# A decoder block whose FFN is multiplied by Strassen's seven products: other signs, sums of h made one stage earlier, operands of f made between products

## The chip, the cores and the metric

One core of one Trainium2 chip runs the whole program. The metric is the device time of one execution in microseconds (us). The names of the engines in the rows are PE (TensorE, matrix products), PEld (its weight loads), DVE (VectorE), ACT (ScalarE), POOL (GpSimd) and SP (SyncE, whose queue issues the DMAs here). PSUM is the memory into which PE writes its sums, SBUF the one in which everything else lies.

## What is computed

One decoder layer on a sequence of 1024 tokens with 1024 channels, in float32. An attention branch and an mLSTM branch run on the same normalised input, are gated, added and multiplied with w_out. Then comes the part that the change is about, a dense FFN with 2816 inner channels, and a last norm:

```python
x = x + (jax.nn.sigmoid(ga) * ya + jax.nn.sigmoid(gm) * ym) @ w_out
f = rmsnorm(x, norm2_g)
h = jax.nn.silu(f @ w_ffn_gate) * (f @ w_ffn_up)
x = x + h @ w_ffn_down
out = rmsnorm(x, final_norm_g)
```

## The kernel before

Every product is made exact enough by splitting both operands into a high and a low half (`split`, L71 to L73): ACT rounds the source into the high tile, DVE subtracts it from the source to give the low tile, and PE does three matmuls, high by high, high by low and low by high (`three`, L828 to L831). One matmul is 128x128 by 128x512.

The program goes through stages. Up to about 657 us it does the projections, the two branches and the product with w_out (loop at L762, eight channel blocks j, each in two token halves). Each half is added to x (L772), scaled into a tile of F_ (L773, f without the row factor) and transposed to tokens (`to_tokens`, L713), where the squares for the norm are summed (ACT L732, DVE L734) and x is written to a DRAM tile x2d.

The FFN uses the Winograd form of Strassen's scheme: a product of two matrices cut into 2x2 quarters is done with seven products in place of eight, at the price of sums and differences of quarters beforehand and of results afterwards.

**Gate and up.** There are 22 pairs n (two channel blocks each; even n are gate, odd n are up). For each pair the seven products run in the order 1, 6, 5, 7, 2, 3, 4 (ORDER, L794). Each is 4 blocks of K by three matmuls, so 12 matmuls, and 84 for a pair. The operands of f for the seven products are 28 tiles z (`f_split` L750, `f_raw` L755, `f_t` L895). They are the same for all pairs and stay resident. Products 1, 2 and 3 take quarters of f as they are; 4, 5, 6 and 7 take differences. Before the first product two of the four K blocks of 1, 2, 3 have been made; everything else, and two passes over differences, stands in the program between the last product with w_out and the first of gate (L915 to L928). The operands of the weights are made 4 products ahead (LA, `prep`, L806): POOL forms four sums per pair (L814), then a split. Weight pairs are loaded by `load_pair` (L800), one pair ahead. Results go out of PSUM by ACT (L867, L875) and DVE (L871, L879, L890); `done` (L842) multiplies by the row factor Rt and applies Silu for gate, multiplies gate by up for up, and stores the quarter of h in the DRAM tile hd_ (L850). The row factor needs rstd2, which comes from the sums of squares (L929 and a power on POOL, L141) and is spread over partitions by PE (`rows_of`, L143).

**Down.** Seven passes over the 11 blocks p, in the order 1, 5, 2, 3, 6, 7, 4 (DORD, L935), 77 steps c of 12 matmuls (4 token blocks t by three). `dload` (L954, 5 steps ahead) fetches quarters of h and of w_dn, `dprep` (L978, 3 steps ahead) forms the sums on POOL (`op`, L984: none in passes 1 and 2, two per step in 5, 3 and 7, one in 6 and 4) and splits the two operands, 512 wide each. Passes 2 and 3 add into the PSUM banks of passes 1 and 5. After each pass the four banks are taken out: ACT copies after 1, 5 and 3; after 2 DVE adds into the rows of x (`add_r`, L1030); after 6 and 7 DVE adds bank and earlier result, POOL adds the next (L1110, L1117). `square` (L1039, ACT) sums squares, `by_g3` (L1058) multiplies by the last norm's weights, `finish` (L1042) takes the power on POOL (L1046) and scales and stores. Pass 4 begins with eight `add_r` on DVE and four `by_g3` on POOL for the second half of the tokens (L1070), and does its last four steps bank by bank.

Instructions are put in order for each engine by the tile framework: among those whose inputs it expects to be there, the one that stands first in the program goes first. On the chip each engine's queue then runs in that order. Tiles of 1024 floats come from one pool `blk` of 37 buffers, half tiles from pools named ev and ws; a tile waits until a buffer has been released.

Of the kernel before, what the change touches and what calls it, by code (L numbers as in the profile page):

```python
# [15 lines left out]
P = 128  # L16
# [16 lines left out]
def hybrid_block(ctx, tc, xT, xt, par, g3row, cst, abias, w_fm, w_mv, w_br, w_o, w_gu, w_dn, out):  # L33
# [675 lines left out]
    hd_ = dr.tile([NF, P, S], F32, name="hd_")  # L709
# [33 lines left out]

    fz = {i: [None] * 4 for i in range(1, 8)}
# [10 lines left out]
    def f_raw(kt):  # L755
        (z11, z12), (z21, z22) = halves(F_[2 * kt]), halves(F_[2 * kt + 1])
        f_split(1, kt, z11)
        f_split(2, kt, z21)
        f_split(3, kt, z22)

    later = []
    for j in range(KD):  # L762
# [6 lines left out]
        g = prm[:, C_G2 + j:C_G2 + j + 1]  # L769
        for h in range(2):  # L770
# [6 lines left out]
        if j in (3, 5):  # L777
            f_raw(j // 2 - 1)
    rstd2 = cp.tile([P, 8], F32, name="rstd2")
    ph_b.close()  # L780
    pC = ctx.enter_context(tc.tile_pool(name="pC", bufs=1))

    def half(name, tag, bufs):
        return pC.tile([P, HALF], F32, name=name, tag=tag, bufs=bufs)

    def bank(s, i):
        if i == 3:
            return st_ps()
        if s == 0:
            return pm.tile([P, HALF], F32, name="mm", tag="mm", bufs=3)  # L790
        return pb.tile([P, HALF], F32, name="mb", tag="mb", bufs=3)


    ORDER = (1, 6, 5, 7, 2, 3, 4)  # L794
    NP2 = NF // 2
    NG7 = 2 * NP2 * 7
    LA = 4
    raws, hl, sums = {}, {}, {}

    def load_pair(n):  # L800

        raws[n] = [blk("wr2") for _ in range(2)]
        for i in range(2):
            nc.sync.dma_start(out=raws[n][i], in_=w_gu[n, i])

    def prep(g):  # L806
        n, i = g // 7, ORDER[g % 7]
        if g % 7 == 0 and n + 1 < 2 * NP2:
            load_pair(n + 1)
        (x11, x12), (x21, x22) = halves(raws[n][0]), halves(raws[n][1])  # L810

        def s_(name, a, b, op):
            sums[name] = half("s_", "ws", 5)
            G.tensor_tensor(sums[name], a, b, op)  # L814
        if i == 6:
            s_(5, x21, x22, ALU.add)
            s_(6, sums[5], x11, ALU.subtract)
        elif i == 7:
            s_(7, x11, x21, ALU.subtract)
        elif i == 3:  # L820
            s_(3, x12, sums[6], ALU.subtract)
        src = {1: x11, 2: x12, 4: x22}
        hi = wp.tile([P, HALF], F32R, name="whi", tag="whi", bufs=5)
        lo = wp.tile([P, HALF], F32R, name="wlo", tag="wlo", bufs=5)
        split(hi, lo, src[i] if i in src else sums[i])
        hl[g] = (hi, lo)
# [6 lines left out]
    def seven(ps, g, more=False):  # L833
        hi, lo = hl.pop(g)
        for kt in range(4):
            c = slice(kt * P, (kt + 1) * P)
            zh, zl = halves(fz[ORDER[g % 7]][kt])
            three(ps, hi[:, c], lo[:, c], zh, zl, kt == 0 and not more, kt == 3, more)

    sg = {}  # L840

    def done(n, ij, c):  # L842
# [9 lines left out]
    def pair(n, also):  # L852
        s, b, e = n % 2, {}, {}
        if s == 0:
            sg.update(enumerate(x for _ in range(2) for x in halves(blk("sg"))))

        def ev(name):
            e[name] = half(name, "ev", 7)
            return e[name]
        for q, i in enumerate(ORDER):  # L860
            g = n * 7 + q
            if g + LA < NG7:
                prep(g + LA)
            if i == 1:
# [49 lines left out]
    for g in range(LA):  # L914
        prep(g)  # L915
# [280 lines left out]
```

## Time and profile before

| | us |
|---|---|
| median of three runs (1390.23 to 1393.22) | 1390.87 |
| the profiled execution | 1392.68 |
| its span, first to last instruction | 1390.9 |
| up to the first product of gate | 657.2 |
| gate and up | 454.6 |
| down, to the last matmul | 271.6 |
| from there to the end | 7.5 |

The page begins with the busy time of each engine and the granted clock of PE in 40 slices of the span. A busy PE is not a PE at its pace: a matmul at the lower clock counts as busy too. So the stages are best read by asking how long they would take if every matmul followed the one before at the full pace, and how much longer they took.

### The profile page before, as it was taken

To read this page: it belongs to the slowest core of one execution; us is meant where nothing else is said; L and a number is where in the kernel's file an instruction comes from. 1 tells how busy PE (TensorE), PEld (TensorE's weight loads), DVE (VectorE), ACT (ScalarE), POOL (GpSimd) and SP (SyncE) were. 2 spreads that over 40 slices of the span, in tenths; PEclk is the share of its full clock that TensorE was granted. 3 is DMA by queue.
4 is the path that set the end of the run, shared out by engine and by line. 5 is a ranking of instruction groups with operands and counts; after the bars stand their busy time and mean duration, and the time that the engine had idled before them with its cause. 6 is when DMAs were issued, how large, how long until landed. Compare 5 with 4: busy or idle time off the path is not lost.

```text
span 1390.9 us, 16876 instructions
## 1 busy us (share of the span) xinstructions
PE 1321.1 (95%) x6090; PEld 1073.8 (77%) x6090; DVE 752.7 (54%) x1290; ACT 571.5 (41%) x1134; POOL 522.0 (38%) x437
## 2 busy tenths in 40 slices
PE   9999999999999999999599999999999998998874
PEld 6888997778888888887488888888888776876653
DVE  6469663565344444334865444544455366656656
ACT  5379863565122222243533333333333243525232
POOL 0245442210000000101465444555455159275966
PEclk9999999999999999999699999999999999998986
DMA  9111011001202111143221222222220295854461
GB/s 336 48 46 32 16 31 61 31 24 33 66 25 60 46 46 54 61 151 127 98 86 61 83 76 92 91 76 91 91 76 32 83 342 173 284 169 146 144 219 61
DMA packets 56964, 134.47 MB, mean 97 GB/s; under 512 B 6449, under 2 KB 6705, under 8 KB 56881
## 3 DMA queue, kind: packets, MB, share of 16 engines
q1 hardware_dynamic: 56880, 133.39, 28.8%
q8 instruction: 48, 0.79, 0.2%
q14 instruction: 36, 0.29, 0.1%
HBM read 113.45 MB, written 19.92 MB: 96 GB/s over the span
## 4 chain that ended last, share of the span: by engine, by line
PE 77%; POOL 7%; DVE 7%; DMA 4%; issue 3%; ACT 1%; SPq 1%; POOLq 0%; ACTq 0%; DVEq 0%
PE mm L108 7%; PE mm L110 7%; PE mm L109 7%; PE mm L830 5%; PE mm L831 5%; PE mm L829 4%; PE mb L830 4%; PE mb L831 4%; PE mb L829 4%; PE mb L110 4%; PE mb L109 4%; PE mb L108 4%; PE st L829 3%; PE st L830 3%; PE st L831 3%
## 5 line engine op out<-in xcount | busy, mean ns | idle before, releaser
L108 PE MATMUL mm<-uh,whi 128*128 128x512 f32 x352 | 140.0, 400 | 0.9 <-ACT whi L72 0.9
L110 PE MATMUL mm<-uh,wlo 128*128 128x512 f32 x352 | 139.0, 395 | 0.0
L109 PE MATMUL mm<-ul,whi 128*128 128x512 f32 x352 | 138.7, 394 | 0.0
L72 ACT ACTIVATE whi<-wraw 128x512 fp32r<-128x512 f32 (+1 forms) x100 | 61.7, 628 | 159.4 <-PE mb L109 99.8
L829 PE MATMUL mm<-z,whi 128*128 128x512 f32 x220 | 88.3, 402 | 7.9 <-ACT z L72 7.9
L880 POOL TENSOR_TENSOR w<-w,d 128x512 f32<-128x512 f32 x22 | 35.3, 1605 | 153.3 <-DVE w L879 147.2
L901 POOL TENSOR_TENSOR t__5803<-f 128x512 f32<-128x512 f32 x1 | 1.3, 1304 | 242.0 <-ACT f L773 242.0
L830 PE MATMUL mm<-z,whi 128*128 128x512 f32 x220 | 88.2, 402 | 3.2 <-DVE z L73 3.2
L831 PE MATMUL mm<-z,wlo 128*128 128x512 f32 x220 | 87.6, 399 | 0.0
L831 PE MATMUL mb<-z,wlo 128*128 128x512 f32 x220 | 86.7, 394 | 0.0
L830 PE MATMUL mb<-z,whi 128*128 128x512 f32 x220 | 86.7, 394 | 0.0
L829 PE MATMUL mb<-z,whi 128*128 128x512 f32 x220 | 86.7, 394 | 0.0
L72 ACT ACTIVATE whi<-wr 128x512 fp32r<-128x512 f32 x66 | 41.5, 629 | 94.7 <-PE st L830 40.9
L108 PEld LDWEIGHTS mm<-uh,whi 128*128 128x128 f32 x352 | 66.3, 188 | 17.0 <-ACT whi L72 2.1
L110 PEld LDWEIGHTS mm<-uh,wlo 128*128 128x128 f32 x352 | 66.2, 188 | 15.5 <-DVE wlo L73 0.2
L109 PEld LDWEIGHTS mm<-ul,whi 128*128 128x128 f32 x352 | 66.3, 188 | 14.4
L73 DVE TENSOR_TENSOR wlo<-wraw,whi 128x512 fp32r<-128x512 f32 (+1 forms) x72 | 48.8, 688 | 51.7 <-ACT whi L72 51.7
L73 DVE TENSOR_TENSOR wlo<-wr,whi 128x512 fp32r<-128x512 f32 x66 | 53.0, 804 | 42.1 <-ACT whi L72 42.1
L830 PE MATMUL mm<-xz 128*128 128x512 f32 x132 | 56.3, 427 | 18.7 <-DVE xz L73 18.7
L829 PE MATMUL st<-z,whi 128*128 128x512 f32 x176 | 70.4, 400 | 0.0
L830 PE MATMUL st<-z,whi 128*128 128x512 f32 x176 | 69.9, 397 | 0.0
L831 PE MATMUL st<-z,wlo 128*128 128x512 f32 x176 | 69.7, 396 | 0.0
(653 smaller groups left out, 3644.1 us busy)
## 6 DMA issues: line engine op xcount, KB each, us to landing
wr<-in_w_gu_dram SPq DMA_DIRECT2D x44, 512.0 KB, 3.8
ld<-in_w_dn_dram SPq DMA_DIRECT2D x88, 256.0 KB, 3.6
wraw<-in_w_fm_dram SPq DMA_DIRECT2D x28, 512.0 KB, 3.6
ld<-hd__5018 SPq DMA_DIRECT2D x55, 256.0 KB, 3.9
hd__5018<-sg SPq DMA_DIRECT2D x44, 256.0 KB, 2.2
xr<-in_xT_dram SPq DMA_DIRECT2D x14, 512.0 KB, 3.7
xt<-in_xt_dram SPq DMA_DIRECT2D x8, 512.0 KB, 7.5
wraw<-in_w_br_dram SPq DMA_DIRECT2D x16, 256.0 KB, 2.7
```

What stands on the lines that cost most here:

```text
L72: A.activation(hi, src, AF.Copy)
L73: eng.tensor_tensor(lo, src, hi.bitcast(F32), ALU.subtract)
L108: T.matmul(ps, ah, bh, start=(i == 0), stop=False)
L109: T.matmul(ps, ah, bl, start=False, stop=False)
L110: T.matmul(ps, al, bh, start=False, stop=(i == n - 1))
L829: T.matmul(ps, xh, zh, start=start, stop=False, skip_group_check=more)
L830: T.matmul(ps, xh, zl, start=False, stop=False, skip_group_check=more)
L831: T.matmul(ps, xl, zh, start=False, stop=stop, skip_group_check=more)
L880: G.tensor_tensor(e["w"], e["w"], e["d5"], ALU.add)
L901: eng.tensor_tensor(ts_[k, kt], a, b, ALU.subtract)
```

## The change

Signs are turned so that other quarters become differences: products 1, 2 and 3 of gate and up still take quarters of f, 5 takes z11 - z12, 6 that plus z22, 4 takes z21 minus that, 7 takes z12 - z22, all made in place in F_. The weights' four POOL sums per pair are all additions now.

The operands of f are made in another place. Of the K blocks 0 to 2, those for products 1 and 5 are made during the product with w_out (`f_even`), the last block of 1 too. Behind it come the last block of 5 and the four of 6; those of 7, 2, 3 and 4 are made two at a time after the first eight products. The first two pairs are interleaved: their products 1 and 5, then 6 and 7, then 2, 3 and 4 follow each other pair by pair. Pair 0 is loaded during the last block of w_out. The rows of rstd2 are spread after product 7 of pair 0, in place of a spot before its `done`.

The sums of h that down needs are formed once when a quarter set is finished (`h_sums`): three on POOL, one on DVE, and all seven operands are stored, each quarter 128x512. `done` gives one more product to DVE and no longer stores the second quarter. In down each step loads one operand of h, ready made, beside one or two quarters of w_dn; POOL does one sum per step in passes 5, 6, 7 and 4, ACT one copy in 5 and 6. Both operands lie in one tile of 1024, which is split at once. Loads are 6 steps ahead and operands 4. The first four are loaded and made during the last products of up. After passes 6 and 7 all sums are on DVE; `by_g3` is gone, and `finish` does scale and weight in one DVE instruction for each half.

```diff
-    hd_ = dr.tile([NF, P, S], F32, name="hd_")
+    hd_ = dr.tile([7, NF // 2, P, HALF], F32, name="hd_")
...
+    def f_even(kt):
+        z11, z12 = halves(F_[2 * kt])
         f_split(1, kt, z11)
-        f_split(2, kt, z21)
-        f_split(3, kt, z22)
+        f_t(5, kt, z11, z11, z12, ALU.subtract)
+
+    def f_t(i, kt, dst, a, b, op):
+        (V if kt % 2 else G).tensor_tensor(dst, a, b, op)
+        f_split(i, kt, dst)
...
+    SEQ = [(n, i) for i2 in ((1, 5), (6, 7), (2, 3, 4)) for n in range(2) for i in i2]
+    SEQ += [(n, i) for n in range(2, 2 * NP2) for i in ORDER]
     LA = 4
...
+        if j == KD - 1:
+            load_pair(0)
+            prep(0)
+            prep(1)
         for h in range(2):
             ps = proj(wt, m_, KD, h)
...
-        if j in (3, 5):
-            f_raw(j // 2 - 1)
+        if j % 2 == 1 and j < 6:
+            f_even(j // 2)
+        elif j == 6:
+            f_split(1, 3, F_[6][:, 0:HALF])
...
+    def h_sums(p, h):
+        x11, x21, x12, x22 = (h[k] for k in range(4))
+
+        def s_(i, a, b, op, eng):
+            t = half("hs", "hs", 3)
+            eng.tensor_tensor(t, a, b, op)
+            h_store(p, i, t)
+            return t
+        s_(7, x11, x21, ALU.subtract, G)
+        s1 = s_(5, x21, x22, ALU.subtract, G)
+        s2 = s_(6, s1, x11, ALU.subtract, G)
+        s_(3, x12, s2, ALU.add, V)
...
-            (V if ij == 0 else G).tensor_tensor(dst, c, dst, ALU.mult)
-            nc.sync.dma_start(out=hd_[n // 2 * 2 + ij // 2, :, hs(ij % 2)], in_=dst)
+            (V if ij in (0, 2) else G).tensor_tensor(dst, c, dst, ALU.mult)
+            h_store(n // 2, {0: 1, 1: None, 2: 2, 3: 4}[ij], dst)
...
+    for kt in range(4):
+        f_rest(6, kt)
+    prep(2)
+    prep(3)
+    rest = [(i, kt) for i in (7, 2, 3, 4) for kt in range(4)]
+    for g, (n, i) in enumerate(SEQ):
+        if g + LA < len(SEQ):
+            prep(g + LA)
+        product7(n, i)
+        if g == 0:
+            to_tokens(*later.pop(0))
+            V.tensor_tensor(rstd2, ss2[:, 0], ss2[:, 1], ALU.add)
+            rstd_of(rstd2, rstd2, D, NT)
+        if n == 2 * NP2 - 1 and i in (7, 2, 3):
+            for c in {7: range(LP), 2: range(2), 3: range(2, LP)}[i]:
+                (dload if i == 7 else dprep)(c)
+        for _ in range(2):
+            if rest:
+                f_rest(*rest.pop(0))
...
-    LD, LP = 5, 3
+    LD, LP = 6, 4
...
+        if i == 5:
+            G.tensor_tensor(t_at(p), *tm, ALU.add)
+            A.activation(z, t_at(p), AF.Copy)
         elif i == 6:
-            x, z = at("sS", p), op(at("sT", p), r[0], at("sT", p))
+            G.tensor_tensor(t_at(p), tm[0], t_at(p), ALU.add)
+            A.activation(z, t_at(p), AF.Copy)
         elif i == 7:
-            x, z = op(None, at("x11", p), r[0]), op(None, r[1], r[2])
-        else:
-            x, z = r[0], op(None, r[1], at("sT", p))
+            G.tensor_tensor(z, *tm, ALU.add)
+        elif i == 4:
+            G.tensor_tensor(z, tm[0], t_at(p), ALU.add)
+        hi, lo = blk("xzh", F32R), blk("xzl", F32R)
+        split(hi, lo, t)
...
+    def finish(t):
         ss = ss3[t]
         rs = ss[:, 3:4]
-        (V if fin else G).tensor_scalar(rs, ss[:, 0:1], ss[:, 1:2], EPS, ALU.add, ALU.add)
+        V.tensor_scalar(rs, ss[:, 0:1], ss[:, 1:2], EPS, ALU.add, ALU.add)
         G.tensor_tensor(rs, rs, nhalf[:, 0:1], ALU.pow)
         for d in range(2):
             x_ = xo[t][:, hs(d)]
-            if not fin:
-                G.tensor_scalar(x_, x_, rs, 1.0, ALU.mult, ALU.mult)
...
+            V.scalar_tensor_tensor(x_, x_, rs, g3[:, hs(d)], ALU.mult, ALU.mult)
             nc.sync.dma_start(out=out[0, t * P:(t + 1) * P, hs(d)], in_=x_)
...
+        elif i == 6:
+            v, c12 = e[1][t], e[3][t]
+            V.tensor_tensor(v, ps, v, ALU.add)
+            V.tensor_tensor(c12, c12, v, ALU.subtract)
+            add_r(t, 1, c12)
+            square(t, 1)
+            if t > 0:
+                finish(t - 1)
+        elif i == 7:
+            w, c22 = e[1][t], e[5][t]
+            V.tensor_tensor(w, ps, w, ALU.add)
+            V.tensor_tensor(c22, c22, w, ALU.subtract)
+            add_r(t + 4, 1, c22)
+            add_r(t + 4, 0, w)
+            square(t + 4, 1)
+        else:
+            add_r(t + 4, 0, ps)
+            square(t + 4, 0)
+            finish(t + 4)
```

## Rows read from the trace of the kernel before

**Rows 1.** The page: busy time of the engines, and PE's granted clock.

```profile
PE 1321.1 (95%) x6090; PEld 1073.8 (77%) x6090; DVE 752.7 (54%) x1290; ACT 571.5 (41%) x1134; POOL 522.0 (38%) x437
...
PEclk9999999999999999999699999999999999998986
```

**Rows 2.** Busy time by stretch: length, PE, PEld, DVE, ACT, POOL (instructions), clock, DMA share, GB/s.

```profile
657.20:694.00 36.80, 20.31 (x70) 14.71 (x69) 31.93 (x46) 20.27 (x42) 20.74 (x12) 0.68 0.27 99
694.00:1111.80 417.80, 417.80 (x1802) 337.99 (x1801) 206.69 (x280) 136.87 (x235) 209.98 (x145) 1.00 0.24 79
1111.80:1383.50 271.70, 231.37 (x925) 181.81 (x924) 174.52 (x185) 104.55 (x195) 180.15 (x135) 0.91 0.57 193
```

**Rows 3.** PE's timeline: start, length, engine, line, operation; first and last products of stages.

```profile
657.22 0.48 PE L829 MATMUL mm<-z,whi 128*128 128x512 f32 x1
...
1089.40 0.39 PE L829 MATMUL mm<-z,whi 128*128 128x512 f32 x1
...
1108.89 0.40 PE L829 MATMUL mb<-z,whi 128*128 128x512 f32 x1
...
1111.44 0.40 PE L831 MATMUL mb<-z,wlo 128*128 128x512 f32 x1
...
1120.65 0.39 PE L829 MATMUL mm<-xz 128*128 128x512 f32 x1
...
1123.39 0.40 PE L829 MATMUL mm<-xz 128*128 128x512 f32 x1
...
1383.00 0.39 PE L831 MATMUL st<-xz 128*128 128x512 f32 x1
```

**Rows 4.** What PE waited for after 657 us: us in total, times, longest.

```profile
PE mm L830 <- DVE xz L73: 18.7, 5, 14.1
PE mm L829 <- ACT xz L72: 13.0, 3, 8.0
PE mm L829 <- ACT z L72: 7.9, 1, 7.9
PE st L146 <- POOL rstd L141: 5.4, 1, 5.4
PE mb L829 <- ACT xz L72: 4.3, 2, 2.4
PE mb L830 <- DVE xz L73: 3.9, 5, 1.2
PE mm L830 <- DVE z L73: 3.2, 2, 2.2
```

**Rows 5.** DVE and POOL alone (timelines), then both beside each other (a stretch).

```profile
1369.46 0.68 DVE L73 TENSOR_TENSOR xz<-tm,xz 128x512 fp32r<-128x512 f32 x1
1370.06 0.68 DVE L73 TENSOR_TENSOR xz<-ld,xz 128x512 fp32r<-128x512 f32 x1
...
1239.98 11.22 POOL L984 TENSOR_TENSOR sT<-ld,sT 128x512 f32<-128x512 f32 x9 [0.42 <-DMA ld<-in_w_dn_dram]
...
1353.00:1366.10 13.10, 0.77 (x4) 0.28 (x2) 13.10 (x9) 5.49 (x13) 13.10 (x9) 0.61 0.00 0
```

**Rows 6.** Timelines at the entry to gate: a sum of squares on DVE, the power on POOL.

```profile
661.66 1.75 DVE L734 CUSTOM_DVE_ANT_0 junk<-x 128x512 f32<-128x512 f32 x1
...
681.69 4.43 POOL L141 TENSOR_TENSOR rstd<-rstd,nhalf 128x8 f32<-128x8 f32 x1 [5.61 <-DVE rstd L140]
```

**Rows 7.** Busy time by stretch: pass 5 of down (columns as in group 2).

```profile
1145.00:1180.00 35.00, 32.00 (x134) 24.65 (x132) 21.59 (x16) 12.36 (x22) 34.37 (x23) 1.00 0.55 180
```

**Rows 8.** Groups by line: a low half 1024 wide (busy us, mean ns, idle before).

```profile
L73 DVE TENSOR_TENSOR ml<-mg,mh 128x1024 fp32r<-128x1024 f32 x8 | 9.8, 1226 | 9.1 <-ACT mh L72 9.1
```

**Rows 9.** DMA issues: size, median us from issue to landing.

```profile
ld<-in_w_dn_dram SPq DMA_DIRECT2D x88, 256.0 KB, 3.6
```

**Rows 10.** Timelines behind the last matmul: the last square on ACT, the last power on POOL.

```profile
1384.27 0.63 ACT L1039 ACTIVATE junk<-xo 128x512 f32<-128x512 f32 x1 [2.05 <-DVE xo L1030]
...
1386.02 0.55 POOL L1046 TENSOR_TENSOR ss<-ss,nhalf 128x1 f32<-128x1 f32 x1 [0.75 <-DVE ss L1045]
```

More of the change, by code (lines that the diff above doesn't have):

```diff
@@ new lines, in hybrid_block, with load_pair, pair_raw @@
+    LA = 4
+    raws, hl, sums = {}, {}, {}
+    def load_pair(n):
+        raws[n] = [x for i in range(2) for x in pair_raw(n, i)]
+    def pair_raw(n, i):
+        if n == 0 and i == 1:
+            r = [half("wr", "ev", 6) for _ in range(2)]
+            for k in range(2):
+                nc.sync.dma_start(out=r[k], in_=w_gu[n, i, :, hs(k)])
+            return r
+        r = blk("wr2") if i else wp.tile([P, 1024], F32, name="wraw", tag="wraw", bufs=2)
+        nc.sync.dma_start(out=r, in_=w_gu[n, i])
+        return halves(r)
@@ new lines, in prep, with s_ @@
+    def prep(g):
+        n, i = SEQ[g]
+        if n and i == 6 and n + 1 < 2 * NP2:
+            load_pair(n + 1)
+        x11, x12, x21, x22 = raws[n]
+        def s_(k, a, b):
+            sums[n, k] = half("s_", "ws", 5)
+            G.tensor_tensor(sums[n, k], a, b, ALU.add)
+        if i in (5, 6) and (n, 5) not in sums:
+            s_(5, x21, x22)
+        if i == 6:
+            s_(6, sums[n, 5], x11)
+        elif i == 7:
+            s_(7, x11, x21)
+        elif i == 3:
+            s_(3, x12, sums[n, 6])
+        src = {1: x11, 2: x12, 4: x22}
+        hi = wp.tile([P, HALF], F32R, name="whi", tag="whi", bufs=5)
+        lo = wp.tile([P, HALF], F32R, name="wlo", tag="wlo", bufs=5)
+        split(hi, lo, src[i] if i in src else sums[n, i])
+        hl[n, i] = (hi, lo)
@@ L848, in done @@
         else:
[L849 to L855 removed]
+            (V if ij in (0, 2) else G).tensor_tensor(dst, c, dst, ALU.mult)
+            h_store(n // 2, {0: 1, 1: None, 2: 2, 3: 4}[ij], dst)
+    sgs, bks, evs = {}, {}, {}
@@ L857, in ev, with product7 @@
+    def product7(n, i):
+        s = n % 2
+        b, e = bks.setdefault(n, {}), evs.setdefault(n, {})
+        if i == 1 and s == 0:
+            sg = [x for _ in range(2) for x in halves(blk("sg"))]
+            sgs[n] = sgs[n + 1] = sg
+        sg = sgs[n]
+        k = {1: 0, 2: 0, 6: 1, 7: 2, 4: 2, 5: 3, 3: 3}[i]
+        more = i in (2, 3, 4)
+        if not more:
+            b[k] = bank(s, k)
+        seven(b[k], n, i, more)
         def ev(name):
-            e[name] = half(name, "ev", 7)
+            e[name] = half(name, "ev", 6)
@@ L935, in hybrid_block @@
     DORD = (1, 5, 2, 3, 6, 7, 4)
     NC_ = 7 * NP2
[L937 to L952 removed]
+    LD, LP = 6, 4
+    draw, dop, sT, dtm = {}, {}, {}, {}
```

322 lines of the change are left out of this document (98 added, 224 removed).

## The prediction

> **What bounds the kernel now.** The first view is the page's busy line. PE is busy for 95% of the span, so no other engine bounds the whole, and only what PE loses can be won [rows 1]. The clock row says that the loss is local: full clock through the whole first half, a dip at the entry to gate and more of them in the last ten slices [rows 1]. The second view is the busy time by stretch. Gate and up from 694 us on is perfect: 417.8 us of 417.8 busy, clock 1.00, with DVE at 206.7 and POOL at 210.0, half free. The entry before it (clock 0.68, PE 20.3 of 36.8) and down (clock 0.91, PE 231.4 of 271.7) are not [rows 2].
>
> To price the loss I need PE's pace. Two matmuls 84 apart in gate and up, the starts of product 4 of the last two pairs, lie 1108.89 - 1089.40 = 19.49 us apart: 19.49 for a pair, 2.78 for a product. In down twelve matmuls take 1123.39 - 1120.65 = 2.74 [rows 3]. Gate and up run from 657.2 to 1111.8, 454.6 us, and at that pace need 22 x 19.49 = 428.8: **25.8 lost**. Down ends at 1383.00 + 0.39 = 1383.4, 271.6 us for 77 x 2.74 = 211.0: **60.6 lost** [rows 3]. Behind the last matmul 7.5 remain. Check: 657.2 + 428.8 + 25.8 + 211.0 + 60.6 + 7.5 = 1390.9, the span.
>
> The third view, PE's waits, splits the loss. At the entry PE stands for 7.9 + 5.4 + 3.2 = 16.5 us, for operands z and for the power of rstd2; in down for 18.7 + 13.0 + 4.3 + 3.9 = 39.9, all for split operands xz [rows 4]. The rest, 9.3 and 20.7, is PE running at half clock (1.2 in place of 2.4 GHz) after such waits, so about half a us for each us stood still.
>
> Why operands are late is seen on DVE and POOL. Alone, low halves on DVE follow each other every 0.60 us, POOL's sums every 11.22 / 9 = 1.25. In the stretch 1353.0 to 1366.1, where both run without a gap, each does about eight, one of each in 1.68 [rows 5]. So beside POOL a DVE instruction that reads two operands from SBUF goes at a third of its pace, and a POOL sum adds 1.68 - 0.60 = **1.08 us** to DVE's work. In pass 5 POOL is busy 34.4 of 35 us: with two sums per step (22 x 1.25 to 1.68 = 27 to 37 us against 30.1 of PE) it is the bound there [rows 7].
>
> **The change part by part.** *Matmuls.* 22 x 84 and 77 x 12 as before: 428.8 + 211.0, no change.
>
> *Entry.* What had to be made between the last product with w_out and product 1 no longer stands there. Products 1 and 5 of two pairs have their operands, up to one K block, before: 4 x 2.78 = 11.1 us of PE work at once, where PE stood 7.9 us after one product's beginning. The power (4.43) [rows 6] is wanted after the sixth product, not the fourth. The work itself does not shrink, it must now fit under the products up to the eleventh (4 of pair 0), whose operand comes last. DVE, two-operand: 4 sums of squares, 7 differences, 21 low halves of z, 9 of weights = 41 x 0.60 = 24.6. POOL: 6 differences, 6 sums of weights, 4 in results = 16 x 1.08 = 17.3, and the power 4.4. Together 46.3; up to 5.2 of it (5 on DVE, 2 on POOL) can run before the stage begins, as buffers of m come free. Cover: ten products 27.8, sixteen narrow matmuls (a quarter of 0.23 each) 0.9, and 2.1 of the eleventh until its last K block: 30.8. Serially that leaves 10.3 to 15.5 us over. The other bound is DVE alone, 24.6 and some nine results out of PSUM at 0.60, 30.0: nothing over. The sum of squares at 1.75 and DVE busy 31.9 of 36.8 say that the serial end is nearer [rows 2, 6]; but POOL is not always busy. I take 7 of waiting and 3 of half clock: **10 lost** (0 to 18), 15.8 won. Moved DMAs: on SP pair 0's weights go ahead of the stage, hidden. Pair 1's first half needs the wraw buffer of the last x block, free after L772, and shares SP with x2d's stores; at about 4 us to land it is there some 5 us in, its split at 6.5, against need at 2 x 2.78 + 0.9. That is inside the 7.
>
> *Sums of h.* Per two pairs POOL gets three sums more and gives one product to DVE, DVE gets one sum: POOL 16 instructions for 14, 16 x 1.08 + 18 two-operand ones on DVE x 0.60 = 28.1 of 39.0 us. With operands made 4 products (11.1 us) ahead this is **0**. The added wait: the sum for 3 on DVE waits for POOL's third, and the low halves of the next weights are queued behind it; 3 x 1.68 = 5.0 us, under the 11.1. Without that cover it would cost up to 5.7 a round (a rival below). Three more stores a round on SP are 0.8 MB in 39 us: nothing, at 79 GB/s now [rows 2].
>
> *Entry to down.* The first four steps are prepared during the last products of up, so PE need not wait for loads and splits at 1112; **1** is left for a surprise (0 to 4).
>
> *Passes 1 to 3, 5, 6.* POOL has 11 sums in passes 5 and 6 and none in 1 to 3. Per step a split of 1024 is 1.23 on DVE [rows 8] (pitch about 1.15) + 1.08 = 2.2 under 2.74. ACT adds a copy, idle enough (104.6 of 271.7) [rows 2]. Loads: three quarters of 256 KB in passes 5 and 7, 0.79 MB in 2.74 us = 287 GB/s, 3.6 to land [rows 9] with six steps ahead. So **0** lost (to 4), where pass 5 alone lost 3 of waiting.
>
> *Pass 7.* After pass 6 DVE has, per token block, a result from PSUM 0.60, its difference 0.60, `add_r` and two scalings 0.67 each: 3.2, in all 12.8, of which 10.4 is two-operand. They stand in the program before the fifth step's split, as the eight `add_r` of pass 4 do now, behind which PE stood its longest wait of 14.1 [rows 4]. They begin 2.1 us before pass 7 and end at 10.7, or, with six POOL sums beside them (6.5), at 17.2; then the split 1.15 to 2.2. Step five is due at 4 x 2.74 = 11.0. So the wait is 0.9 to 8.4; I take **5**.
>
> *Pass 4.* DVE after pass 7: 0.60 + 0.60 + 2 x 0.67 = 2.5 a block, 10.2, ending at 8.1 to 14.6, the split at 9.3 to 16.8 against 11.0 if the lead of four steps is whole. After pass 7 it isn't: it comes back at 2.74 - 2.2 = 0.5 a step, some 3.5 us. So 0 to 13; I take **6**, below today's 14.1 as `by_g3` and POOL's part of the sums are gone.
>
> *Clock.* 11 us of waits, half a us each as above: **5**. Down loses 1 + 5 + 6 + 5 = **17** (4 to 36), 43.6 won.
>
> *End.* square, scalar, power, scaling, store stay in a row [rows 10]; one scaling of 0.67 more on DVE, one `by_g3` of 0.7 less: **0**.
>
> Sum: 657.2 + 428.8 + 10 + 211.0 + 17 + 7.5 = 1331.5, which is 59.4 below the span of 1390.9. The profiled execution took 1392.68 in all, 1.8 around the span, so the changed kernel's would take 1333.3; the median of the runs is 1.8 below the profiled one, hence **1331.5** there.
>
> Of the sharing of DVE and POOL the Trainium skill says, in "SBUF — State Buffer", section "Who interferes with whom", that a DVE instruction with two SBUF inputs and a GpSimd instruction that reads SBUF exclude each other for a whole instruction. The row's 1.68 for a pair is nearly its sum, 1.85, so the trace mostly agrees. By the rule a POOL sum would cost DVE 1.25 in place of 1.08, in the entry and passes 7 and 4 (16 + 22 instructions) up to 6.5 us more, 1338.
>
> **The rivals.** *Nearly all is hidden.* DVE's queue order turns out well (splits between the results), the waits shrink to 3 at the entry and 6 in down: 1313.5. For it: POOL has half of its down work left. Against: DVE still has 12.8 us ahead of a lead of 11.
>
> *DVE and POOL serial all over.* The entry takes its 15.5 with clock, 18, and down the upper ends 8.4 + 13, 11 of half clock and 4 for loads and start, 36: 657.2 + 428.8 + 18 + 211.0 + 36 + 7.5 = 1358.5. For it: the stretch at 1353. Against: POOL runs dry when its loads are late.
>
> *The interleaving does not do what it says.* Pair 1's weights land late or the differences stand in DVE's queue ahead of its split; entry as before, 25.8: 1347.
>
> *Slower.* The sum for 3 on DVE stands behind POOL's chain each round. POOL's queue holds a product and weights' sums too, so if DVE is held for longer than the splits are ahead, PE stands. It decides when the hold passes 11.1 us; the price is then that of a hold not covered, 5.7 or more a round, 11 rounds 63: 1331.5 + 63 = 1394.5. For it: DVE's queue is in order. Against: POOL half idle there [rows 2].
>
> **How the numbers follow.** Forecast, 1320 to 1344: 0.58. All hidden 0.17, interleaving idle 0.07, serial 0.13, slower 0.05. The range leaves out half of the best case and the upper half of the serial one with the slower: 1312 to 1358. A difference of 0.2% is about what a measurement of this kernel can tell from none. Faster 0.94, same 0.01, slower 0.05.
>
> **What would show it.** Right: PE's first product of gate at about 657 with eleven us and no wait behind it, waits for z in the ten products after; gate and up at 19.49 a pair with no waits; down without waits until its sixth pass, then one at pass 7's and one at pass 4's fifth step, both released by DVE's low half behind `add_r`. Wrong: waits for xz in passes 1 to 6 (loads, buffers), waits of PE in gate and up every 39 us, or POOL full in any pass.

## The result, and the profile after

The changed kernel takes **1333.42 us** (median of four runs, 1331.28 to 1334.98), the kernel before 1392.01 beside it: a ratio of 0.958, 95% interval 0.956 to 0.960. The forecast was 1331.5, range 1312 to 1358. The profiled execution took 1331.28, with a span of 1329.5, so it is the quickest of the four; of before it lies 0.7 above the median. So spans differ by 61.4 where medians differ by 58.6, and 2.8 us have to be kept in mind in every comparison of spans below.

The page of the kernel after: busy time of the engines, and PE's granted clock in 40 slices.

```profile
PE 1303.4 (98%) x6090; PEld 1066.1 (80%) x6090; DVE 765.0 (58%) x1261; ACT 572.7 (43%) x1078; POOL 458.5 (34%) x374
...
PEclk9999999999999999999989999999999999999989
```

Against [rows 1]: the same 6090 matmuls, POOL down from 522 to 458 us with 63 instructions fewer, DVE up by 12. The dips of the clock in the last ten slices are nearly gone.

Busy time by stretch of the kernel after, columns as in [rows 2]: the entry to gate, the rest of gate and up, and down; then passes 5, 7 and 4 of down.

```profile
657.00:690.00 33.00, 27.73 (x118) 22.36 (x117) 31.73 (x42) 20.03 (x40) 21.69 (x14) 0.90 0.33 112
690.00:1094.00 404.00, 404.00 (x1744) 327.12 (x1743) 242.16 (x301) 138.99 (x237) 240.29 (x160) 1.00 0.31 105
1094.00:1322.00 228.00, 220.52 (x938) 177.56 (x936) 145.24 (x130) 101.89 (x135) 82.63 (x54) 0.99 0.67 228
...
1131.00:1161.00 30.00, 30.00 (x132) 24.37 (x131) 18.41 (x11) 15.97 (x21) 21.27 (x14) 1.00 0.93 328
1253.00:1288.00 35.00, 31.11 (x122) 24.43 (x121) 32.47 (x32) 12.75 (x18) 23.83 (x16) 0.90 0.72 257
1288.00:1322.00 34.00, 30.41 (x131) 24.08 (x129) 25.42 (x31) 10.75 (x20) 6.21 (x5) 1.00 0.11 38
```

At the entry the clock is 0.90 where it was 0.68, and DVE has as much work as before (31.7 us) in 33.0 us in place of 36.8. In down POOL has 82.6 us of work in place of 180.2, and pass 5, where POOL was the bound [rows 7], now has PE busy 30 of 30. Only pass 7, with DVE busy 32.5 of 35, still looks crowded.

All that PE waited for after 640 us in the kernel after (us in total, times, longest), to be read against [rows 4]; then those waits, and the first and last products of the stages, on PE's timeline.

```profile
PE mb L856 <- DVE xzl L73: 3.9, 2, 3.1
PE mm L146 <- DVE v L916: 3.4, 1, 3.4
PE mm L856 <- DVE xzl L73: 2.2, 1, 2.2
PE mb L857 <- DVE wlo L73: 1.8, 1, 1.8
```

```profile
657.30 0.48 PE L855 MATMUL mm<-z,whi 128*128 128x512 f32 x1
...
665.84 0.67 PE L857 MATMUL mb<-z,wlo 128*128 128x512 f32 x1 [1.83 <-DVE wlo L73]
...
681.79 1.13 PE L146 MATMUL mm<-idn,rstd 128*128 128x128 f32 x8 [3.45 <-DVE v L916]
...
1097.04 0.40 PE L855 MATMUL mm<-xzh 128*128 128x512 f32 x1
...
1249.70 0.39 PE L855 MATMUL mb<-xzh 128*128 128x512 f32 x1
...
1264.82 0.50 PE L856 MATMUL mb<-xzl,xzh 128*128 128x512 f32 x1 [0.81 <-DVE xzl L73]
...
1270.95 0.79 PE L856 MATMUL mb<-xzl,xzh 128*128 128x512 f32 x1 [3.08 <-DVE xzl L73]
...
1287.47 0.39 PE L855 MATMUL mm<-xzh 128*128 128x512 f32 x1
...
1301.23 0.50 PE L856 MATMUL mm<-xzl,xzh 128*128 128x512 f32 x1 [2.23 <-DVE xzl L73]
...
1320.26 0.39 PE L857 MATMUL st<-xzh,xzl 128*128 128x512 f32 x1
```

Of 56.4 us of waiting 11.4 are left, in five waits. The account by the prediction's own ideals: gate and up take 1097.04 - 657.30 = 439.7, so 10.9 lost (25.8 before); down takes 1320.65 - 1097.04 = 223.6, 12.6 lost (60.6 before); 8.85 remain behind the last matmul (7.5 before). The gain is 14.9 + 48.0 - 1.35 = 61.5 of span, with 0.1 lost ahead of 657 [rows 3].

Down can also be taken apart by pass, from a pass's first matmul to the next one's. Undisturbed, a pass takes 30.5 us. The start with pass 1 went from 36.0 to 30.6, pass 5 from 36.9 to 30.5, pass 6 from 42.8 to 30.5, pass 4 from 57.0 to 33.2; passes 2 and 3 were undisturbed before, and pass 7 takes 37.8 in both. So of the 48.0 won pass 4 gave 23.8, pass 6 12.3, pass 5 6.3 and the start 5.4. Pass 4 has the longest wait of before, 14.1, pass 6 the second longest; PE's timeline of before in pass 6, to the start of pass 7:

```profile
1245.80 0.39 PE L829 MATMUL mm<-xz 128*128 128x512 f32 x1
...
1256.72 0.80 PE L829 MATMUL mm<-xz 128*128 128x512 f32 x1 [7.96 <-ACT xz L72]
...
1288.63 0.40 PE L829 MATMUL mb<-xz 128*128 128x512 f32 x1
```

### The profile page after: what moved, and what is told of

Its sections match the earlier page's. It is cut to its first block, busy times and chain, and to the rows that moved or that the text cites. A ratio compares the mean times of both kernels' runs of the same rounds, so it can differ in the third digit from the quotient of the medians.

```text
span 1329.5 us, 16764 instructions
## 1 busy us (share of the span) xinstructions
PE 1303.4 (98%) x6090; PEld 1066.1 (80%) x6090; DVE 765.0 (58%) x1261; ACT 572.7 (43%) x1078; POOL 458.5 (34%) x374
## 3 DMA queue, kind: packets, MB, share of 16 engines
q1 hardware_dynamic: 61776, 142.05, 31.7%
## 4 chain that ended last, share of the span: by engine, by line
PE 87%; DVE 7%; issue 2%; ACT 1%; DMA 1%; POOL 1%; SPq 0%; DVEq 0%; POOLq 0%; ACTq 0%
PE mm L108 8%; PE mm L110 7%; PE mm L109 7%; PE mm L856 6%; PE mm L857 6%; PE mm L855 6%; PE mb L856 5%; PE mb L857 5%; PE mb L855 5%; PE st L857 4%; PE st L855 4%; PE st L856 4%; PE mb L110 4%; PE mb L109 4%; PE mb L108 4%
## 5 line engine op out<-in xcount | busy, mean ns | idle before, releaser
L72 ACT ACTIVATE whi<-wraw 128x512 fp32r<-128x512 f32 (+1 forms) x144 | 89.3, 628 | 221.3 <-PE mb L109 99.8
L73 DVE TENSOR_TENSOR xzl<-ld,xzh 128x1024 fp32r<-128x1024 f32 x77 | 110.4, 1463 | 69.3 <-ACT xzh L72 62.0
L73 DVE TENSOR_TENSOR wlo<-wraw,whi 128x512 fp32r<-128x512 f32 (+1 forms) x116 | 88.6, 771 | 76.4 <-ACT whi L72 75.5
L72 ACT ACTIVATE xzh<-ld 128x1024 fp32r<-128x1024 f32 x77 | 79.7, 1056 | 58.5 <-DMA ld<-in_w_dn_dram 24.9
L855 PE MATMUL mm<-z,whi 128*128 128x512 f32 x220 | 86.7, 394 | 0.0
L856 PE MATMUL mm<-z,whi 128*128 128x512 f32 x220 | 86.7, 394 | 0.0
L890 ACT ACTIVATE sg<-sg 128x512 f32<-128x512 f32 x44 | 27.7, 629 | 88.1 <-DVE sg L889 49.9
```

Source lines behind the costliest of these rows:

```text
L72: A.activation(hi, src, AF.Copy)
L73: eng.tensor_tensor(lo, src, hi.bitcast(F32), ALU.subtract)
L855: T.matmul(ps, xh, zh, start=start, stop=False, skip_group_check=more)
L856: T.matmul(ps, xh, zl, start=False, stop=False, skip_group_check=more)
L890: A.activation(dst, dst, AF.Silu)
```

## The experiments

The theory: the entry gains because operands are made behind the products and the interleaving gives them time; down gains because POOL's sums no longer stand beside DVE, and what waits are left in passes 7 and 4 are DVE's results from PSUM standing ahead of the next low halves, slowed by POOL. The rivals: a longer lead, the early start, or other order does it. Where nothing else is said, each kernel is the one after with the edit shown; times are medians of four runs, to be compared with 1333.42 (before: 1392.1 to 1392.7 beside them). Profiles of equal kernels start the first product of gate anywhere from 656.4 to 659.4, the wait for the rows of rstd2 is 3.5 or 5.0 us, and that of pass 4 between 2.2 and 5.0 in five kernels that leave pass 4 as it is. So 2 us between two profiles say nothing.

**One pair at a time.**

```diff
-    SEQ = [(n, i) for i2 in ((1, 5), (6, 7), (2, 3, 4)) for n in range(2) for i in i2]
-    SEQ += [(n, i) for n in range(2, 2 * NP2) for i in ORDER]
+    SEQ = [(n, i) for n in range(2 * NP2) for i in ORDER]
...
-        for _ in range(2):
+        for _ in range(3):
             if rest:
```

> The changed kernel without the interleaving: the products follow each other pair by pair, and the rest of the operands of f is made three at a time so that each is there before its product. If the cover of two pairs' products is what pays for the operands (theory), those of products 2, 3 and 4 are due four to seven products (11 to 19 us) earlier and the entry, which loses 10.9 us in the changed kernel, loses 18 to 25: 1341 to 1348 us. If only the moving of the work behind the first product counts and the interleaving is idle (rival), it stays within 2 us of 1333.4.

1337.05 us (1335.12 to 1337.39), 3.6 more, between the theory's range and the rival's. Gate and up take 443.8 and lose 15.0 in place of 10.9; the kernels with the entry of after take 439.4 to 440.9 there. PE's longest wait there:

```profile
685.45 0.80 PE L855 MATMUL st<-z,whi 128*128 128x512 f32 x1 [4.46 <-DVE z L73]
```

It is an operand of f that is late, as the theory says, but the size is smaller than it said: the interleaving is worth some 4 of the 14.9 us won at the entry. (The edit also makes product 6 the second of each pair, and the rest of the operands three at a time, so the 4 are the price of all this.) By elimination the other 11 come from what both versions have: the operands of the first products made earlier, and the rest behind products and not ahead of them. No run parts these two.

**The first products' weights first, and the rows of rstd2 in another bank.** Two edits of order at the entry, one kernel each.

```diff
-    for kt in range(4):
-        f_rest(6, kt)
     prep(2)
     prep(3)
+    for kt in range(4):
+        f_rest(6, kt)
```

> Only the order at the entry: the operands of the third and fourth product's weights stand in the program ahead of the four differences of product 6. Theory (the 1.8 us wait for pair 1's low weight half is a place in DVE's queue): the wait goes and 2 to 3 us with it, 1330 to 1332. Rival (the load of pair 1 lands when it lands, and the later waits for z and the rows take over): 1333 to 1335, with more waiting at 672 to 698 us.

```diff
-  rows_of(Rt[:, hs(h)], rstd2, h * 4, pm.tile([P, HALF], F32, name="mm", tag="mm", bufs=3))
+  rows_of(Rt[:, hs(h)], rstd2, h * 4, pb.tile([P, HALF], F32, name="mb", tag="mb", bufs=3))
```

> The changed kernel with the rows of rstd2 spread through a free bank of the other pair's set (mb) in place of mm, whose only free one waits for DVE to take product 6 of pair 0 out. PE waits 3.45 us there. Theory: that wait is the bank's and falls to under 0.5, with its half clock 4 to 6 us less: 1328 to 1330. Rival: DVE is behind with operands anyway, so the wait only moves to the next product that needs z: within 2 us of 1333.4, with a new wait for DVE's low half of z between 683 and 700 us.

The first gave 1335.57 (1332.84 to 1336.68), with the same wait of 1.8 at the same place. DVE, ACT and POOL run the instructions of the entry in the same order as in the kernel after, so the edit did not reach these engines, and whether the low half's place in DVE's queue makes the wait was not tested. What this run does show is that the medians of two kernels that run the entry alike can lie 2.1 us apart.

The second gave 1333.79 (1332.19 to 1335.44): the wait of 3.45 is gone, and five of 0.55 to 0.84 for low halves of z, 3.4 in all, stand behind it. The rival holds: DVE is busy 31.7 of 33 us there in the kernel after, and with one wait taken away others come. In this profile gate and up take 437.8, some 2 us less than in the kernels with the entry of after; the median does not show it.

**POOL's sums put back.** 44 more POOL instructions beside the same loads in passes 5, 3 and 7, each a multiplication with one in place, ahead of the step's split.

```diff
+        if i in (3, 5, 7):
+            G.tensor_tensor(t[:, 0:HALF], t[:, 0:HALF], one, ALU.mult)
+        if i == 3:
+            G.tensor_tensor(z, z, one, ALU.mult)
```

> The changed kernel with as many POOL instructions per step of down as before: in passes 3, 5 and 7 POOL multiplies ready operands by one (two more in pass 3, one more in 5 and 7, 44 in all), ahead of the split, so nothing else of order, loads or sums changes. If POOL's load was the bound of down (theory), pass 5 is again bound by it (22 instructions at 1.25 to 1.68 against 30.5 us of PE) and pass 7's wait grows by 11 x 1.08: down, 223.6 us in the changed kernel, grows by 10 to 25: 1343 to 1358 us. If down got faster through the longer lead, the early first steps or the queue orders (rival), it grows by less than 4.

1350.38 us (1348.61 to 1351.5), 17.0 more; down takes 241.4, 17.8 more. PE's two longest waits:

```profile
1280.08 0.80 PE L856 MATMUL mb<-xzl,xzh 128*128 128x512 f32 x1 [7.58 <-DVE xzl L73]
...
1319.88 0.79 PE L856 MATMUL mm<-xzl,xzh 128*128 128x512 f32 x1 [8.39 <-DVE xzl L73]
```

The same low halves as in the kernel after, in passes 7 and 4, later by 4.5 and 6.2 us (the second by less against the longer waits of pass 4 in other profiles). POOL's load costs what the theory said in all, but not where it said: pass 5, which it expected POOL to bound, takes 30.6 us, with POOL busy 26.2 of 30, and pass 6 30.5. The 17.8 are 4.0 in pass 2, 2.1 in pass 3, 3.9 in pass 7 and 7.8 in pass 4. In pass 7 the way to PE is a queue: POOL's power for a scaling starts only at 1269.64, behind its products and sums, and DVE stands for it with the late low half behind:

```profile
1270.24 1.41 DVE L1064 SCALAR_TENSOR_TENSOR xo<-xo,ss,g 128x512 f32<-128x512 f32 x2 [4.20 <-POOL ss L1061]
```

**The same sums taken out of the kernel before.** This is the reverse test: `before` with `x, z = r[0], ...` in passes 5, 3 and 7, which leaves a part of the product out and saves one load a step in pass 5.

```diff
-            x = op(r[0], r[0], r[1], ALU.add)
-            z = op(r[2], r[2], r[3])
+            x, z = r[0], op(r[1], r[1], r[2])
...
-            s2 = op(at("sS", p), at("sS", p), at("x11", p))
-            x, z = op(None, r[0], s2), r[1]
+            x, z = r
...
-            x, z = op(None, at("x11", p), r[0]), op(None, r[1], r[2])
+            x, z = r[0], op(None, r[1], r[2])
```

> The kernel before with one thing left out: the 44 POOL sums of h in passes 5, 3 and 7 of down (a quarter of h is used as it was loaded, so part of the product isn't computed; two loads fewer a step in pass 5 by one). The sums per step are then those of the kernel after, the order of the results is that of before. Theory (the number of POOL instructions beside DVE makes most of down's loss): of the 60.6 us lost in down 30 to 45 go, 1347 to 1362, what stays being the waits behind the results ahead of passes 7 and 4. Rival (the 17 us that putting them into the kernel after cost is their whole price; the other 30 of down's gain is order and lead): 1373 to 1378.

1375.42 us (1371.28 to 1378.14) beside 1392.6: 17.2 less. The rival's time holds: two opposite tests give 17 us for the sums of h, not 30 to 45. But they are not the same 17 us. Here pass 5 is cured (PE 35.00 of 35, POOL 7.62 of 35, against [rows 7]; 30.5 us in place of 36.9), and so is pass 6 (30.6 in place of 42.8), the two passes in which POOL's work put back cost nothing. Pass 7 takes 2.4 less; pass 4 takes 4.9 more and the start 1.0 more. Down still takes 256.7 and loses 45.7. The first matmuls of passes 6 and 7 in this kernel, and two of its three longest waits (the third is 3.67 at the seam); then the timelines of POOL and of SP's queue ahead of the first of these waits, and of DVE ahead of the second:

```profile
1241.36 0.40 PE L829 MATMUL mm<-xz 128*128 128x512 f32 x1
...
1271.94 0.39 PE L829 MATMUL mb<-xz 128*128 128x512 f32 x1
...
1324.12 0.79 PE L829 MATMUL mm<-xz 128*128 128x512 f32 x1 [8.31 <-ACT xz L72]
...
1356.84 0.80 PE L830 MATMUL mm<-xz 128*128 128x512 f32 x1 [15.15 <-DVE xz L73]
```

```profile
1322.14 1.26 POOL L984 TENSOR_TENSOR tm<-ld,sT 128x512 f32<-128x512 f32 x1 [4.53 <-DMA ld<-in_w_dn_dram]
```

```profile
1312.28 5.69 SPq L1053 DMA_DIRECT2D out_dram<-xo  x4
1318.02 0.45 SPq L959 DMA_DIRECT2D ld<-in_w_dn_dram  x1
```

```profile
1353.37 1.75 DVE L1028 SCALAR_TENSOR_TENSOR xo<-a,rstd,xo 128x512 f32<-128x512 f32 x1
1355.04 1.74 DVE L73 TENSOR_TENSOR xz<-tm,xz 128x512 fp32r<-128x512 f32 x1
```

The wait of 8.3 begins on SP: the stores of finished rows wait there for POOL's scalings (the last two run from 1316.25 to 1317.6), and the next quarter of w_dn is queued behind them, issued only at 1318.02. The wait of 15.2 is the eight `add_r` at 1.7 us each beside POOL. The 3.7 at the seam is a start without operands. Of these three, 27.1 us of waiting, that of 8.3 is new; the other two stand in before as well (14.1 and 3.65). So the gain is a balance: in this profile, the slowest of the four, 21 us less in passes 5, 6 and 7, and 6 more at the start and in pass 4.

**Order alone in the kernel before.** The eight `add_r` and four `by_g3` of pass 4 go between its steps.

```diff
                 load_x2(t)
-                add_r(t, 1, e["d5"][t - 4])
-                add_r(t, 0, e["v"][t - 4])
-                square(t, 1)
-                by_g3(t, 1, G)
...
             dop.pop(c)
+            if i == 4 and p in (0, 2, 4, 6):
+                t = 4 + p // 2
+                add_r(t, 1, e["d5"][t - 4])
                add_r(t, 0, e["v"][t - 4])
                square(t, 1)
                by_g3(t, 1, G)
```

> The kernel before with one thing changed: the eight add_r and four products with the norm's weights ahead of pass 4 are spread over its steps 1, 3, 5 and 7. Theory (order alone holds the longest wait, 14.1 us and its half clock): 15 to 22 us less, 1370 to 1377, with all other waits as they were. Rival (POOL's sums of pass 4 still come beside them and the lead is eaten up after pass 7, so the wait moves to other steps): 1384 to 1392.

1392.77 us (median of ten, 1390.9 to 1394.48) beside 1392.6: nothing. The wait of 14.1 [rows 4] is there in other pieces, the largest being 6.0 and 5.0; the first of them, and two `add_r` on DVE's timeline:

```profile
1362.15 0.80 PE L830 MATMUL mm<-xz 128*128 128x512 f32 x1 [5.99 <-DVE xz L73]
```

```profile
1362.01 1.76 DVE L1030 SCALAR_TENSOR_TENSOR xo<-d,rstd,xo 128x512 f32<-128x512 f32 x1
1363.69 1.75 DVE L1030 SCALAR_TENSOR_TENSOR xo<-a,rstd,xo 128x512 f32<-128x512 f32 x1
```

POOL still has its sums of results, of w_dn and the products of `by_g3` there, without a gap from 1352 to 1368, and nearly every `add_r` and low half beside them takes 1.7 us. In this stretch both engines are full, and order alone gains nothing.

**No POOL sums in passes 7 and 4 of the kernel after.** Their operand of w_dn is one quarter as loaded, so a part of the product is left out.

```diff
-            dtm[c] = ld(1, 1), ld(0, 1)
+            ld(1, 1, z), ld(0, 1)
...
-            dtm[c] = (ld(1, 0),)
+            ld(1, 0, z)
...
-        elif i == 7:
-            G.tensor_tensor(z, *tm, ALU.add)
-        elif i == 4:
-            G.tensor_tensor(z, tm[0], t_at(p), ALU.add)
```

> The changed kernel without POOL's sums in passes 7 and 4 (22 instructions): those operands of w_dn are one quarter as loaded, so this part of the product is left out; the loads stay, all else too. PE waits 0.8 and 3.1 us in pass 7 and 2.2 in pass 4. If the sharing of DVE and POOL makes these waits (forecast's term: up to six sums beside the results, 6.5 us), both fall to under 0.5 and with their half clock 7 to 10 us go: 1323 to 1327. If it is DVE's order alone (12.8 and 10.2 us of results ahead of the splits against 11 to 13.9 of lead), the wait in pass 7 stays over 1.5.

1322.31 us (1321.78 to 1322.73), 11.1 less and a little under the theory's range, and no wait of PE in down. So the waits of passes 7 and 4 need POOL's share. Whether it acts by slowing DVE (the low halves take 1322 ns in the mean in place of 1463) or by having the operand ready later, this run does not tell apart.

**DVE's results of passes 7 and 4 spread over the steps**, POOL's sums as they are.

```diff
-            if t > 0:
-                finish(t - 1)
...
-            w, c22 = e[1][t], e[5][t]
-            V.tensor_tensor(w, ps, w, ALU.add)
-            V.tensor_tensor(c22, c22, w, ALU.subtract)
-            add_r(t + 4, 1, c22)
-            add_r(t + 4, 0, w)
-            square(t + 4, 1)
+            pend.append((t, ps))
...
+            if i == 7 and p in (1, 3, 5, 7):
+                finish(p // 2)
+            if i == 7 and p in (2, 4, 6, 8):
+                load_x2(p // 2 + 3)
+            if i == 4 and p in (0, 2, 4, 6):
+                second(*pend.pop(0))
```

> The changed kernel with DVE's other work of passes 7 and 4 spread between the steps: the scalings after pass 6 come behind the splits of steps 6, 8, 10 and of the first of pass 4, the results of pass 7 behind those of steps 5, 7, 9 and 11; the rows of x are loaded between too. POOL's sums stay. If the waits come from results standing ahead of splits in DVE's queue (theory), both vanish though POOL shares as before, 7 to 10 us less: 1323 to 1327. If the sharing is what counts, more than half of the waits stays.

**1321.52 us** (1321.18 to 1322.77), ratio 0.949 to before (0.948 to 0.951): 11.9 us quicker than the kernel after, beyond the theory's 7 to 10, and level with the kernel without those sums. All that PE waits for after 640 us in it:

```profile
PE mm L146 <- DVE v L916: 5.0, 1, 5.0
PE mb L857 <- DVE wlo L73: 1.8, 1, 1.8
```

Down has no wait here either. The waits of the kernel after need both causes, DVE's block of results and POOL beside it, and either one removed ends them. What order could not do in the kernel before it does here, where POOL is idle for most of pass 4 (6.2 us of 34). The two tests of order differ in more than that: this one also spreads the scalings over pass 7, and has a step more of lead and no `by_g3`.

**The lead back to 5 and 3.**

```diff
-    LD, LP = 6, 4
+    LD, LP = 5, 3
```

> The changed kernel with the lead of before in down: loads 5 steps ahead in place of 6, operands 3 in place of 4. If the waits at the head of passes 7 and 4 are DVE's results queued ahead of the splits (theory), each grows by one step, 2.75 us, and half a us of half clock for each us: plus 5 to 9, 1338 to 1342. If buffers of the pool limit the lead anyway (rival), nothing changes, within 2 us of 1333.4; if the lead carried down's gain, plus 15 or more.

1336.2 us (1335.48 to 1338.49), 2.8 more, where the two kernels that run the entry alike differ by 2.1. The waits in pass 7 grow from 3.9 to 5.0, where a step less of lead would be 2.7; that in pass 4 is 4.5, inside its spread. The intervals of the two ratios overlap (0.958 to 0.961 here, 0.956 to 0.960 after), so the step of lead is worth between nothing and 3 us, less than the theory's 5 to 9, and far from carrying down's gain.

**No early start of down.**

```diff
-        if n == 2 * NP2 - 1 and i in (7, 2, 3):
-            for c in {7: range(LP), 2: range(2), 3: range(2, LP)}[i]:
-                (dload if i == 7 else dprep)(c)
...
-    for c in range(LP, LD):
+    for c in range(LD):
         dload(c)
+    for c in range(LP):
+        dprep(c)
```

> The changed kernel with the first steps of down loaded and prepared after the last product of up, as before. The kernel before stood 3.65 us there and ran at half clock for 3.3 us after it. Theory: plus 3 to 6, 1336 to 1339 us, all at the seam. Rival: the order that the framework gives loads them early by itself, plus 0 to 1.

1334.66 us (1333.36 to 1335.79), and no wait at the seam. The rival holds: the program's place for the first loads makes no difference, since the framework issues them early in either case (here DVE makes the first low half of down at 1082.66, 14.6 us before down begins). Why the kernel before stood 3.65 us there is seen on SP's queue in its trace: what SP waited for from 1079 to 1115, and the first loads of w_dn, which stand behind those stores:

```profile
SPq L850 <- POOL sg L849: 31.2, 3, 26.5
```

```profile
1111.62 0.92 SPq L959 DMA_DIRECT2D ld<-in_w_dn_dram  x2
```

Stores of h waited there for POOL's products, and the loads came out only when gate and up had ended. No run moved these stores alone.

**The end's scalings one block later.**

```diff
             add_r(t + 4, 0, ps)
             square(t + 4, 0)
-            finish(t + 4)
+            if t > 0:
+                finish(t + 3)
+            if t == 3:
+                finish(7)
```

> The changed kernel with the scaling of each last token block placed behind the next block's addition. Behind the last matmul the changed kernel takes 8.85 us, 1.4 more than forecast, as the last addition stands behind a scalar of the block before that waits for ACT. Theory: 1.0 to 1.5 us less behind the last matmul, 1332. Rival: the framework orders by its own expectation and nothing moves.

1333.88 us (1332.74 to 1334.91): nothing, 9.1 us behind the last matmul.

**All four changes of order together**, the diffs of the spread results, the weights first, the rows' bank and the end as shown above.

> Four changes of order together: the results of passes 7 and 4 spread over their steps (alone 1321.5), the rows of rstd2 in a bank of their own, the weights of pairs 1's next products ahead of the four differences of product 6, and the tail's scalings one block later. Theory (the entry and the tail have 3 to 5 us of waits that order alone can take away once DVE's rows are no longer held by a bank): 1317 to 1320. Rival (at the entry DVE is behind with operands whatever stands first, and the tail is a chain; only the spread results count): 1321 to 1323.

1322.24 us (1321.41 to 1324.02), no better than the spread results alone. The rival holds. At the entry 10.7 us are lost as before, with the low half of the weights 1.9 late and three waits of 0.7 to 0.8 for z; the end has grown to 10.0 us, because the last `add_r` now stands behind a scaling:

```profile
1314.59 0.75 DVE L1057 SCALAR_TENSOR_TENSOR xo<-xo,ss,g 128x512 f32<-128x512 f32 x1 [0.66 <-POOL ss L1054]
1315.26 0.75 DVE L1043 SCALAR_TENSOR_TENSOR xo<-st,rstd,xo 128x512 f32<-128x512 f32 x1
```

Its bank was ready at 1312.24.

## Why the prediction was right, step by step

The sum of the span came out 2.0 too long, as its terms were off by +0.9 at the entry, -4.4 in down, +1.35 at the end and 0.1 ahead, which partly cancel. The median came out 1.9 above the forecast all the same, since the profiled run of after lies 2.1 below its median where the prediction assumed 1.8 above. That both are within 2 us is in part luck.

**Entry, 10 forecast, 10.9 measured.** Of it 5.3 are waits (forecast 7), 4.2 half clock (1.7 behind the first wait, 2.5 behind the second; forecast 3) and 0.9 the narrow matmuls of the rows, which the prediction counted as cover and left out of the loss; 0.5 is left over. The serial bound of 10.3 to 15.5 of waiting was not reached, as was argued from POOL's gaps. The first wait is the one foreseen inside the 7, pair 1's low weight half (due 6.5 us in, made 8.5 in); the second was not foreseen: PE's spreading of rstd2 needs a PSUM bank, and the DVE result that empties it (680.97) stands behind a difference of f, two low halves of z and one of weights, which begin at 676.39. The power took 2.02 us in place of 4.43 [rows 6] and was off the path.

**Sums of h, 0 forecast, 0 measured.** The wait that the rival of 1394.5 rests on is there. The group of that DVE sum in gate and up, with the idle time before it:

```profile
L877 DVE TENSOR_TENSOR hs<-sg,hs 128x512 f32<-128x512 f32 x10 | 6.9, 692 | 25.6 <-POOL hs L877 25.6
```

DVE stands 2.6 us a round for POOL's third sum, half the 5.0 that were allowed for, and PE is busy 404.00 of 404.00: four products of cover were enough, and the rival's condition never came.

**Down's start, 1 forecast, 0 measured. Passes 1 to 3, 5 and 6, 0 forecast, no wait measured.** POOL's part had room: the low halves 1024 wide take 1463 ns in the mean against 1226 alone [rows 8]. If the 44 of 77 steps with a POOL sum carry the whole difference, a sum costs DVE 0.237 x 77 / 44 = 0.41 us, not 1.08.

```profile
L73 DVE TENSOR_TENSOR xzl<-ld,xzh 128x1024 fp32r<-128x1024 f32 x77 | 110.4, 1463 | 69.3 <-ACT xzh L72 62.0 <-PE st L857 6.9
```

**The ideal of down is the mis-sized term.** In the spread kernel down takes 213.99 us without one wait: 2.779 a step, the pace of gate and up. The 2.74 that the prediction read off a single step is too quick by 0.04, or 3.0 us in 77 steps, which stood among the losses. So after loses 9.6 in down in truth, 6.1 of waits and 3.5 of half clock, where 12 and 5 were forecast.

**Pass 7, 5 forecast, 3.9 measured. Pass 4, 6 forecast, 2.2 measured** (up to 5.0 in other profiles). The mechanism is the forecast one: results on DVE, then the late low half. From DVE's timeline of the kernel after, the first result of each pass, what stands just before the late low halves, and these:

```profile
1248.32 1.28 DVE L1070 TENSOR_TENSOR e<-mm,e 128x512 f32<-128x512 f32 x2
...
1263.56 1.21 DVE L73 TENSOR_TENSOR xzl<-ld,xzh 128x1024 fp32r<-128x1024 f32 x1
1265.21 3.46 DVE L1057 SCALAR_TENSOR_TENSOR xo<-xo,ss,g 128x512 f32<-128x512 f32 x2 [0.44 <-POOL ss L1054]
1268.59 5.73 DVE L73 TENSOR_TENSOR xzl<-ld,xzh 128x1024 fp32r<-128x1024 f32 x4
...
1286.68 1.28 DVE L1078 TENSOR_TENSOR e<-mb,e 128x512 f32<-128x512 f32 x2
...
1298.63 1.41 DVE L1043 SCALAR_TENSOR_TENSOR xo<-e,rstd,xo 128x512 f32<-128x512 f32 x2
1299.96 3.49 DVE L73 TENSOR_TENSOR xzl<-ld,xzh 128x1024 fp32r<-128x1024 f32 x3
```

In pass 7 the results end 18.9 us after the pass began, later than the 10.7 to 17.2 forecast: three stops of 0.44 for POOL's power and one low half stand among them. PE waits at the sixth and seventh step, not at the fifth, whose low half was made before the results. In pass 4 they end after 12.5 us (8.1 to 14.6 forecast) and the wait is at the fifth step as forecast. The lead, forecast as some 3.5 us when pass 4 begins, was whole again: behind pass 7's results four low halves came every 1.43 us and five more every 2.26, the last at 1286.7, so all four steps of lead stood ready at 1287.47. That is why the wait is shorter than the 6 forecast.

**End, 0 forecast, 1.35 measured.** The step that failed is the 0 for one scaling more on DVE against one `by_g3` less [rows 10]. It counted instructions and not their order:

```profile
1321.90 0.21 DVE L1053 TENSOR_SCALAR ss<-ss 128x1 f32<-128x1 f32 x1 [1.12 <-ACT junk L1048]
1322.03 0.74 DVE L1043 SCALAR_TENSOR_TENSOR xo<-st,rstd,xo 128x512 f32<-128x512 f32 x1
```

The last bank was ready at 1320.65, but its `add_r` stands on DVE behind the scalar of the block before, which waits for ACT's square.

**Why before was slow.** The prediction put down's loss on DVE and POOL sharing, with pass 5 and the longest wait as its places. By pass the 48 us lay in pass 4 (23.8), pass 6 (12.3), pass 5 (6.3) and the start (5.4). Passes 5 and 6 are shown to be the sums of h: without them before runs both at the pace of after. The start is read from the trace alone, as loads on SP behind stores that wait for POOL. Pass 4 has the eight `add_r` beside POOL's results, sums and weights; spreading them did nothing, leaving the sums of h out did not help there, and which of POOL's work there, the order or the lead made up its 23.8 stays open. That two opposite tests both gave 17 us is chance: put back into after, POOL's work costs time in passes 2, 3, 7 and 4, and taken out of before it frees 5, 6 and 7.

A pair of one DVE and one POOL instruction cost 1.68 us again in the kernel before with its results spread (`add_r` at 1362.01 and 1363.69 above; POOL's three products beside them took 5.06), where two `add_r` alone follow each other in 0.67. The Trainium skill's rule in "SBUF — State Buffer", section "Who interferes with whom", that the two exclude each other for a whole instruction, would give 0.67 + 1.25 = 1.92 as an estimate; the measurement decides, and it lies closer to the rule than to no sharing, but below it. The 1338 by the rule was 4.6 us too long.

## What to carry to other kernels

Price an engine's load in the stretch where it meets the other's, and then ask whether order or load is the cause: spreading a block of results gained 11.9 us in a kernel where POOL had time left, and nothing in one where both engines were full. (The two kernels differ in other things too, so take it as a question to ask and not as a law.) Compare two tests pass by pass before saying that they agree: 17 us and 17 us came from different passes. Read the ideal pace over a whole undisturbed stage and not off one step: 0.04 us a step was 3 us of 12.6. A store that waits for a slow engine delays the loads queued behind it, so look at the DMA queue ahead of each late operand. And look whether an edit of order reached the engines before reading its time: one here did not.

## What the runs showed that was not expected

The price of a wait in clock does not follow its length. The first wait at the entry is 1.83 us in the kernel after and 1.82 in the kernel with spread results, at the same matmul. In the first the nine matmuls behind it took 3.75 us where 2.09 would do: most of them follow each other every 0.43 us, the half clock of 1.2 GHz, and the price was 1.7, almost the wait itself. In the second they run on at the full clock, and the price is 0.1. Busy time behind the wait in each, columns as in [rows 2]:

```profile
665.80:670.00 4.20, 4.16 (x11) 3.33 (x12) 4.20 (x5) 2.59 (x6) 3.22 (x2) 0.59 0.59 192
```

```profile
665.70:670.00 4.30, 4.26 (x18) 3.50 (x19) 4.30 (x5) 4.10 (x9) 3.25 (x2) 1.00 0.53 198
```

In the kernel after the wait of 2.23 in pass 4 cost 0.1 as well, and that of 3.08 in pass 7 2.9. So the prediction's half a us for each us of waiting is a mean over many waits. Before, 56.4 us of waiting came with 27 us of other loss in the two stages (3 more are 2.74's making), half a us each. After, 11.4 of waiting came with 4.2 + 3.5 = 7.7 at half clock, 0.7 each.
